# A two-layer diffusion trunk on one core: the large inputs re-laid by the host as the loads read them, and the tokens given transposed

## The chip, the cores and the metric

The kernel runs on one core of one Trainium2 chip. The metric is the device time of one execution in microseconds (us); the kernel before takes 2646.81 us, the median of 3 runs. The core has a matmul engine, TensorE (PE in the profile, with PEld for its weight loads), a vector engine (DVE), a scalar engine (ACT), GpSimd (POOL) and SyncE (SP), which here issues the DMAs. Each of them takes its own instructions in the order in which they were laid down when the program was built.

## The reference

Two layers over 512 latent tokens `x` and 256 context tokens `ctx`, each a vector of 2048. The first ("even") layer holds differential attention (8 heads) and windowed attention with a sink (8 heads), the second ("odd") one attention with normed queries and keys (8 heads) and latent attention (8 heads). Cut to what matters:

```python
silu_c = jax.nn.silu(c); silu_cc = jax.nn.silu(c_ctx)
for l in range(DEPTH):                                   # DEPTH = 2
    mod = silu_c @ w_mod[l] + b_mod[l]                   # 2048 -> 6144, one vector
    shift, scale, gate = jnp.split(mod[:, None, :], 3, axis=-1)
    cmod = silu_cc @ w_mod[l] + b_mod[l]                 # the same for the context
    cshift, cscale, cgate = jnp.split(cmod, 3)
    h = rmsnorm(x, norm_g[l]) * (1.0 + scale) + shift
    hc = rmsnorm(cx, norm_g[l]) * (1.0 + cscale) + cshift
    u, uc = h @ w_in, hc @ w_in                          # e_w_in or o_w_in
    ...                                                  # two groups of attention heads
    y = jnp.concatenate([y1, y2], axis=-1) * jax.nn.silu(ug)
    x = x + gate * (y @ w_o[l])                          # and cx likewise in the first layer
return rmsnorm(x, final_g)
```

## The kernel before

**Layout.** Activations are kept transposed: 2048 features are 16 chunks of 128 partitions, and a chunk is a tile of 128 x 768 whose first 512 columns are the latent tokens and whose last 256 are the context. Each float32 operand of a large product is split into two narrower parts (a cast on ACT, L273 for weights, and a subtraction on DVE, L231), and each row block of a projection is three matmuls (L292, L293, L295), each over 512 and 256 columns. A weight piece goes from DRAM through `wraw` (L278, the load at L282, three buffers of 128 x 1024) and `wsplit` (L265) to `proj` (L297). A load takes a block of 128 columns and up to 8 x 128 rows of a weight as it lies in DRAM, so each contiguous run is 128 floats, 512 bytes.

**Start.** The tokens come as rows of x and ctx: 24 loads of 128 x 512 (L321), 2 KB a row. ACT squares each and sums it along the row (L324). PE transposes the tiles, 96 blocks of 128 x 128 (L331), and DVE copies them out of PSUM into the 16 transposed tiles `xT` (L334, L336). Those are also written to the scratch tensors `x0d` in DRAM, two of them early (L339) and 14 at the end of the start (L429), since the residual of the first layer is read from there (`out_chunk`, L698). From the sums comes the reciprocal root (L342 to L344), which `spread` (L239) turns, by matmuls with the identity (L236), into a row `rs0` that all partitions hold.

**Modulation.** `mod_first(k)` (L131) makes scale and shift of chunk k of the first layer on PE: w_mod comes in pieces of 128 columns (L149, 512 bytes a row), 32 matmuls (L153) on four column groups of the array, a copy on ACT (L160), and two tiny matmuls (L163) that add up the groups; DVE adds the bias (L122, L126). It runs two chunks ahead of the loop at L415, which for each chunk makes the normed and modulated input (`make_h`, L383: the product with rs0 on POOL or DVE, h on ACT L390, an affine step on DVE L393, and the lower part l by L231) and does 24 matmuls of the first four projection blocks. Chunk 0's modulation waits for nothing but its loads. All other gates, scales and shifts come from `mod_later` (L168), in the background: 128 loads of 128 x (2 x 512) of w_mod (L175, 2 KB a row), multiplied and summed on DVE (L186), ACT (L181, L183) and POOL (L184), and folded by PE (L194) with narrow matmuls. `tick` (L223) lets a few of its 128 pieces go between the heads. Its raw tiles `mraw` have two buffers.

**Order.** The source gives the order of dependencies; when the program is built, a scheduler picks from what is ready and so sets each engine's order. All loads and stores go through SP's queue in the order of their issue; a DMA whose buffer is still being read holds those behind it.

**Later norms.** In `out_chunk` ACT squares the new tokens (L710), POOL adds them up (L715), and `rstd_cols` (L251) sums over the partitions by matmuls against a column pair of ones (L256), six for a 128 x 768 tile. The last part of the odd layer has `d_pe` (L868), with two loads of 64 columns, and the shared rotary key (L861), a projection of 64 columns that is written to both halves of the partitions.

Of the kernel before, what the change touches and what calls it, by code (L numbers as in the profile page):

```python
# [9 lines left out]
F32 = mybir.dt.float32  # L10
# [7 lines left out]
P = 128  # L18
# [14 lines left out]
O_G0 = 2368  # L33
# [8 lines left out]
def trunk_kernel(ctx: ExitStack, tc: tile.TileContext, T):  # L42
# [39 lines left out]
    x0d = [dr.tile([P, TOK], F32, name=f"x0d{j}") for j in range(NCH)]  # L82
# [36 lines left out]
    def mod_finish(l, k0, nk, src, nv=2):  # L119
        """adds the bias to chunks k0.. of the modulation; the scale becomes (1 + scale) * norm_g"""  # L120
# [10 lines left out]
    def mod_first(k):  # L131
        """scale and shift of one chunk of the first layer on the tensor engine"""
        acc = pst.tile([P, 512], F32, name="T")
        for sec in range(2):
            col = D_MODEL * (1 - sec) + 128 * k
            at = 0
            while at < NCH:
# [6 lines left out]
                else:  # L144
# [4 lines left out]
                last_raw[0] = nc.sync.dma_start(rv, T["w_mod"][0][128 * at:128 * (at + n), col:col + P]  # L149
                                                .rearrange("(k p) c -> p k c", p=P))  # L150
# [82 lines left out]
    def spread_to(dst, cols, ts):  # L233
        """per-token columns (every other one) to a row that every partition holds"""
# [16 lines left out]
    def rstd_cols(accs, ts, dim, name, bank=jbank):  # L251
        """1 / rms over the partitions, one column pair for each tile of tokens"""
# [12 lines left out]
    def wsplit(rv, nk, cols=P):  # L265
        """the rows of a loaded weight piece, each as an exact sum of two narrower parts"""
        res = []
        for k0 in range(0, nk, 4):
# [3 lines left out]
            for c in range(0, P, cols):  # L272
                nc.scalar.copy(wh[:, :n, c:c + cols], rv[:, k0:k0 + n, :])  # L273
                sub(wl[:, :n, c:c + cols], rv[:, k0:k0 + n, :], wh[:, :n, c:c + cols])
# [3 lines left out]
    def wraw(src, nk, cols=P, raw=None):  # L278
# [3 lines left out]
        nc.sync.dma_start(rv, src.rearrange("(k p) c -> p k c", p=P))  # L282
# [14 lines left out]
    def proj(w, col, xs=None, lat_only=False, cols=P, at=(0, 512)):  # L297
# [4 lines left out]
        for k0 in range(0, n, 8):  # L302
            nk = min(8, n - k0)
            ws = wsplit(wraw(w[128 * k0:128 * (k0 + nk), col:col + cols], nk, cols), nk, cols)
# [5 lines left out]
    def xrows(t, d0):  # L310
        if t < 4:
            return T["x"][0, 128 * t:128 * t + 128, d0:d0 + 512]
        return T["ctx"][0, 128 * (t - 4):128 * (t - 4) + 128, d0:d0 + 512]

    ssx = const.tile([P, 6, 4], F32, name="ssx")
    xT = []
    for dg in range(4):
        xt = []
        for t in range(6):
            a = hslot("xin", F32)[:, 0:512]  # L320
            nc.sync.dma_start(a, xrows(t, 512 * dg))  # L321
            xt.append(a)
            sq = sp["ep"].tile([P, 512], F32, tag="sqA", name="sqx", bufs=1)
            nc.scalar.activation(sq, a, AF.Square, accum_out=ssx[:, t, dg:dg + 1])  # L324
        for i in range(4):
            k = 4 * dg + i
            xk = hslot("xT", F32) if k == 0 else tmp("xT") if k == 1 else slot("xT") if k < 12 else (oslot if k < 14 else sgslot)("xT")
            for t0, t1 in ((0, 4), (4, 6)):
                tp = psj.tile([P, 512], F32, name="J")
                for t in range(t0, t1):  # L330
                    nc.tensor.transpose(out=tp[:, 128 * (t - t0):128 * (t - t0) + 128],  # L331
                                        in_=xt[t][:, 128 * i:128 * i + 128], identity=ident)
                if t0 == 0:
                    nc.vector.tensor_copy(xk[:, 0:512], tp)  # L334
# [6 lines left out]
    rsv = rsx.rearrange("p (a b) -> p a b", b=2)[:, :, 0]
    nc.vector.reduce_sum(rsv, ssx, axis=AX.X)  # L342
    nc.scalar.activation(rsv, rsv, AF.Sqrt, bias=epsc, scale=1.0 / D_MODEL)
    nc.vector.reciprocal(rsv, rsv)  # L344
# [3 lines left out]
    # constants of the even layer  # L348
# [34 lines left out]
    def make_h(l, k, xk, rs, xn, first):  # L383
        """normed and modulated input, split; first: which factor is there early, the norm's or the modulation's"""
# [688 lines left out]
```

## Time and profile before

| what | us |
|---|---|
| median of 3 runs | 2646.81 (2646.05 to 2647.2) |
| profiled execution, span | 2642.8 |
| outside the span (median less span) | 4.0 |
| PE busy | 2522.8 (95%) |
| DVE busy | 1653.1 (63%) |
| ACT busy | 1169.6 (44%) |
| POOL busy | 510.7 (19%) |
| first projection matmul | 45.71 |
| last matmul of the start's projections | 177.64 |

The DMA engines moved 303.39 MB at 115 GB/s over the whole span. The profile is a page on one execution, and a trace that can be asked by stretch, line or tile. Its rows give, in this order, the line of the kernel, the engine, the operation, what is written and from what, the count, and then busy us, the mean ns of one, and the idle time before it with what ended it. PEclk is the clock that TensorE was granted, 1.0 being full. A float32 matmul shows as two records in the timeline. A chain is followed back from the last instruction; here it goes back to about 1154 us and says nothing of the start, which is read from the stretches.

### The profile page before, as it was taken

The numbers are of one execution on the slowest core, as the hardware profiler recorded it, in microseconds if no ns is written. First come the engines' busy times: TensorE is split into PE (matmuls) and PEld (weight loads), VectorE is DVE, ScalarE is ACT, GpSimd is POOL, SyncE is SP. The second block draws the span as 40 slices with busy tenths as digits, with TensorE's granted clock in tenths as the row PEclk, the third lists the DMA queues.
The fourth block names the chain that finished last, engine by engine and source line by source line (L and its number), as shares of the span: only waits on it lengthen the run. The fifth ranks groups of instructions, "written<-read, shape, count | busy, mean of one in ns | idle before, by whom it ended". The sixth has DMA issues, their size and how long they took to land.

```text
span 2642.8 us, 38799 instructions
## 1 busy us (share of the span) xinstructions
PE 2522.8 (95%) x14830; PEld 2124.4 (80%) x14830; DVE 1653.1 (63%) x3199; ACT 1169.6 (44%) x2500; POOL 510.7 (19%) x340
## 2 busy tenths in 40 slices
PE   6989999999999989999998999899999999999998
PEld 4767887888788878888887888688888888777787
DVE  4458666556855688777756665767745336776634
ACT  4234544444544455544444333345434335554433
POOL 0114000001301164443402443310010010000010
PEclk9999999999999999999999999899999999999999
DMA  9993111111311244343443554635622232122334
GB/s 286 279 271 112 47 47 48 47 54 47 112 50 59 64 143 120 108 132 104 130 132 116 181 181 149 193 112 161 186 68 84 68 92 58 51 77 72 88 114 149
DMA packets 394553, 303.39 MB, mean 115 GB/s; under 512 B 18048, under 2 KB 334464, under 8 KB 394368
## 3 DMA queue, kind: packets, MB, share of 16 engines
q1 hardware_dynamic: 394368, 300.93, 38.2%
q8 instruction: 116, 1.90, 0.3%
q14 instruction: 69, 0.57, 0.1%
HBM read 268.64 MB, written 32.24 MB: 114 GB/s over the span
## 4 chain that ended last, share of the span: by engine, by line
PE 47%; DVE 5%; DMA 2%; ACT 1%; issue 1%; POOL 0%; ACTq 0%; SPq 0%; DVEq 0%; POOLq 0%
PE J L292 12%; PE J L295 12%; PE J L293 12%; PE O L579 3%; PE SL L512 3%; PE SC L507 2%; PE T L564 2%; DMA mraw<-in_w_mod_dram 1%; DVE macc L186 1%; DVE l L396 1%; DVE wl L231 1%; PE T L256 0%; PE J L194 0%; POOL macc L184 0%; DVE ptl L231 0%
## 5 line engine op out<-in xcount | busy, mean ns | idle before, releaser
L292 PE MATMUL J<-h,wh 128*128 128x512 f32 (+1 forms) x2224 | 788.3, 357 | 9.4 <-ACT h L390 5.0
L293 PE MATMUL J<-l,wh 128*128 128x512 f32 (+1 forms) x2224 | 769.3, 355 | 4.3 <-DVE l L396 3.4
L295 PE MATMUL J<-h,wl 128*128 128x512 f32 (+1 forms) x2224 | 710.9, 356 | 3.3 <-DVE wl L231 3.3
L231 DVE TENSOR_TENSOR wl<-wraw,wh 128x512 fp32r<-128x512 f32 (+1 forms) x504 | 394.1, 787 | 327.9 <-ACT wh L273 312.0
L273 ACT CAST wh<-wraw 128x512 fp32r<-128x512 f32 (+1 forms) x496 | 302.8, 615 | 536.9 <-PE J L293 471.4
L292 PEld LDWEIGHTS J<-h,wh 128*128 128x128 f32 x2224 | 423.9, 191 | 86.3 <-ACT h L390 6.7
L293 PEld LDWEIGHTS J<-l,wh 128*128 128x128 f32 x2224 | 425.3, 191 | 59.5 <-DVE l L396 4.6
L295 PEld LDWEIGHTS J<-h,wl 128*128 128x128 f32 x2224 | 391.3, 192 | 37.9 <-DVE wl L231 5.1
L184 POOL TENSOR_TENSOR macc<-macc,mraw 128x512 f32<-128x512 f32 x180 | 267.0, 1484 | 266.1 <-ACT mraw L183 233.7
L292 PE MATMUL J<-yh,wh 128*128 128x512 f32 (+1 forms) x800 | 275.1, 351 | 5.2 <-ACT yh L473 4.1
L293 PE MATMUL J<-yl,wh 128*128 128x512 f32 (+1 forms) x800 | 272.4, 351 | 0.2
L186 DVE SCALAR_TENSOR_TENSOR macc<-mraw,silc,macc 128x512 f32<-128x512 f32 x240 | 235.3, 980 | 50.9 <-DMA mraw<-in_w_mod_dram 46.9
L295 PE MATMUL J<-yh,wl 128*128 128x512 f32 (+1 forms) x800 | 252.9, 349 | 0.0
L183 ACT ACTIVATE mraw<-mraw,silc 128x512 f32<-128x512 f32 x180 | 129.8, 724 | 203.0 <-DVE macc L186 178.5
L568 ACT CAST pth<-T 128x256 fp32r<-128x256 f32 (+2 forms) x288 | 125.6, 450 | 149.8 <-PE T L564 146.4
L292 PEld LDWEIGHTS J<-yh,wh 128*128 128x128 f32 x800 | 150.3, 189 | 33.2 <-ACT yh L473 4.9
L231 DVE TENSOR_TENSOR ptl<-T,pth 128x256 fp32r<-128x256 f32 (+2 forms) x288 | 145.4, 516 | 42.9 <-ACT pth L568 40.5
L293 PEld LDWEIGHTS J<-yl,wh 128*128 128x128 f32 x800 | 150.9, 189 | 20.0 <-DVE yl L231 1.1
L523 DVE TENSOR_REDUCE mc<-SC 128x1 f32<-128x256 f32 x208 | 87.3, 420 | 118.4 <-PE SC L507 117.6
L440 POOL TENSOR_TENSOR r<-r,cos 128x512 f32<-128x512 f32 x31 | 40.7, 1313 | 581.9 <-DVE t L439 386.7
L295 PEld LDWEIGHTS J<-yh,wl 128*128 128x128 f32 x800 | 140.2, 190 | 12.4
L538 ACT ACTIVATE e<-SC,nb 128x256 f32<-128x256 f32 x144 | 68.2, 474 | 184.9 <-DVE nb L532 128.8
(297 smaller groups left out, 3789.2 us busy)
## 6 DMA issues: line engine op xcount, KB each, us to landing
mraw<-in_w_mod_dram SPq DMA_DIRECT2D x164, 512.0 KB, 4.1
wraw<-in_e_w_in_dram SPq DMA_DIRECT2D x96, 512.0 KB, 3.8
wraw<-in_w_o_dram SPq DMA_DIRECT2D x62, 512.0 KB, 4.1
wraw<-in_o_w_in_dram SPq DMA_DIRECT2D x62, 512.0 KB, 3.9
mraw<-in_w_mod_dram SPq DMA_DIRECT2D x28, 384.0 KB, 6.3
x0d<-xT SPq DMA_DIRECT2D x16, 384.0 KB, 6.4
res<-x0d SPq DMA_DIRECT2D x16, 384.0 KB, 4.7
xad<-nx SPq DMA_DIRECT2D x16, 384.0 KB, 2.4
```

Source lines behind the costliest of these rows:

```text
L183: nc.scalar.mul(rv[:, i, :], rv[:, i, :], sc)
L184: nc.gpsimd.tensor_tensor(macc[:, v, :], macc[:, v, :], rv[:, i, :], op=ALU.add)
L186: nc.vector.scalar_tensor_tensor(macc[:, v, :], rv[:, i, :], sc, macc[:, v, :], op0=ALU.mult, op1=ALU.add)
L231: nc.vector.tensor_tensor(o, a, h.bitcast(F32), op=ALU.subtract)
L273: nc.scalar.copy(wh[:, :n, c:c + cols], rv[:, k0:k0 + n, :])
L292: nc.tensor.matmul(o, lhsT=wh, rhs=xh[:, c0:c1], start=first and (opens or o is lat), stop=False)
L293: nc.tensor.matmul(o, lhsT=wh, rhs=xl[:, c0:c1], start=False, stop=False)
L295: nc.tensor.matmul(o, lhsT=wl, rhs=xh[:, c0:c1], start=False, stop=last and (closes or o is lat))
L512: nc.tensor.matmul(SL[:, c0:512], lhsT=q, rhs=k[:, 128 * lo:128 * hi], start=(i == 0), stop=(i == n - 1 and not masks))
L523: nc.vector.reduce_max(mc, SC[:, :256], axis=AX.X)
L568: nc.scalar.copy(ph, tv)
L579: nc.tensor.matmul(o, lhsT=v[:, cols[i]], rhs=pt[part][:, i, :], start=(n == 0), stop=(n == len(steps) - 1))
```

## The change

The host now lays the large inputs out as the loads read them, and the loads become plain rows.

- `xT` is the transposed x and ctx, 16 tiles of 128 x 768: 16 loads with rows of 3 KB take the place of 24, and transposes, PSUM copies, row sums and all of `x0d` (two early writes, 14 late ones) go. `out_chunk` reads its residual from `xT`.
- The sums of squares now come from the transposed tiles: ACT squares each (128 x 768) and PE sums it over the partitions with six matmuls against a column pair of ones, 96 in all. Root and reciprocal follow for 12 columns.
- `wm0` holds the modulation's first part by chunk and section, so a piece is a row of 2, 3 or 4 KB; `wm1` holds 128 x 1024 for one piece of `mod_later`, 4 KB a row.
- `_columns` lays `w_o`, `e_w_in`, `o_w_in` and `d_w_q_b` by blocks of 128 columns, so that a load of 8 row blocks has rows of 4 KB and one of 4 row blocks 2 KB; `dkv` has 4 KB.
- The 64 columns of the shared rotary key stand twice in `ow`, so that all pieces have 128 columns and `wsplit`, `wraw` and `proj` lose `cols`; the gates' first column moves from 2368 to 2432. `d_pe` makes one load instead of two.

```diff
-                last_raw[0] = nc.sync.dma_start(rv, T["w_mod"][0][128 * at:128 * (at + n), col:col + P]
-                                                .rearrange("(k p) c -> p k c", p=P))
+                last_raw[0] = nc.sync.dma_start(raw[:, :n * P], T["wm0"][k, sec][:, at * P:(at + n) * P])
...
-                nc.sync.dma_start(rv, T["w_mod"][l][256 * r:256 * r + 256, 512 * b:512 * b + 512]
-                                  .rearrange("(k p) c -> p k c", p=P))
+                nc.sync.dma_start(raw, T["wm1"][b + 4 if l else b - 8, r])
...
-        rv = raw[:, :nk * cols].rearrange("p (k c) -> p k c", k=nk)
-        nc.sync.dma_start(rv, src.rearrange("(k p) c -> p k c", p=P))
-        return rv
+        nc.sync.dma_start(raw[:, :nk * P], w[col // P][:, k0 * P:(k0 + nk) * P])
+        return raw[:, :nk * P].rearrange("p (k c) -> p k c", k=nk)
...
-    ssx = const.tile([P, 6, 4], F32, name="ssx")
-            a = hslot("xin", F32)[:, 0:512]
-            nc.sync.dma_start(a, xrows(t, 512 * dg))
-            nc.scalar.activation(sq, a, AF.Square, accum_out=ssx[:, t, dg:dg + 1])
-                    nc.tensor.transpose(out=tp[:, 128 * (t - t0):128 * (t - t0) + 128],
-                                        in_=xt[t][:, 128 * i:128 * i + 128], identity=ident)
-                    nc.vector.tensor_copy(xk[:, 0:512], tp)
-                    nc.vector.tensor_copy(xk[:, 512:768], tp[:, :256])
-                nc.sync.dma_start(x0d[k], xk)
+    mp = jbank()
+    for k in range(NCH):
...
+        nc.sync.dma_start(xk, T["xT"][k])
+        xT.append(xk)
+        sq = sp["ep"].tile([P, TOK], F32, name="e")
+        nc.scalar.square(sq, xk)
         for t in range(6):
+            nc.tensor.matmul(mp[:, 2 * t:2 * t + 2], lhsT=sq[:, P * t:P * t + P], rhs=ones[:, 0:2],
+                             start=(k == 0 and t == 0), stop=(k == NCH - 1 and t == 5))
...
         load_cs(64)
-        for k in range(2, NCH):
-            nc.sync.dma_start(x0d[k], xT[k])
...
-        nc.sync.dma_start(res, x0d[j])
+        nc.sync.dma_start(res, T["xT"][j])
...
-    kr = roped(*proj(w, D_KPE0, cols=64), 64)
+    kr = roped(*proj(w, D_KPE0), 64)
...
+def _columns(w):
+    r, c = w.shape
+    return np.ascontiguousarray(w.reshape(r // P, P, c // P, P).transpose(2, 1, 0, 3)).reshape(c // P, P, r)
```

How the change stands in the instruction order is seen at three places. First PE at the very start. `cid` holds the identity, `xin` the token rows, `e` (in the third row of after) the squares, `mraw` pieces of w_mod, and `rsx` the reciprocal roots. Before:

```order
L98 MATMUL T<-cid,e 128x89
L101 MATMUL T<-cid,e 128x96
L331 MATMUL J<-cid,xin 128x128 x94
L153 MATMUL T<-mraw_529,sil 32x128 x6
L331 MATMUL J<-cid,xin 128x128 x2
L236 MATMUL J<-cid,rsx 128x128 x4
L153 MATMUL T<-mraw_537,sil 32x128 x6
L236 MATMUL J<-cid,rsx 128x128 x2
```

And after:

```order
L97 MATMUL T<-cid,e 128x89
L100 MATMUL T<-cid,e 128x96
L314 MATMUL J<-ones,e 128x2 x96
L150 MATMUL T<-mraw_398,sil 32x128 x6
L150 MATMUL T<-mraw_406,sil 32x128 x6
L150 MATMUL T<-mraw_414,sil 32x128 x4
L150 MATMUL T<-mraw_420,sil 32x128 x3
L232 MATMUL J<-cid,rsx 128x128 x6
```

The 96 matmuls of the sums stand where the transposes stood, all in one row, and chunk 0's modulation behind them.

Second, DVE at the last chunk of the start: `l0_14` and `l0_15` are the lower parts of chunks 14 and 15, `modc0` the scales and shifts, `macc` the sum of the background modulation. Before:

```order
L231 TENSOR_TENSOR l0_14_1885<-xn_1882,h0_14_1884 128x768
L122 TENSOR_TENSOR modc0_205<-T_1810,bmod_186 128x2 x2
L126 SCALAR_TENSOR_TENSOR modc0_205<-modc0_205,vcol_185 128x2
L393 TENSOR_SCALAR xn_1915<-xn_1915,modc0_205 128x512
L393 TENSOR_SCALAR xn_1915<-xn_1915,modc0_205 128x256
L231 TENSOR_TENSOR l0_15_1918<-xn_1915,h0_15_1917 128x768
```

And after:

```order
L227 TENSOR_TENSOR l0_14_1754<-xn_1751,h0_14_1753 128x768
L182 SCALAR_TENSOR_TENSOR macc_2659<-mraw_2660,silc_177,macc_2659 128x512
L121 TENSOR_TENSOR modc0_189<-T_1679,bmod_170 128x2 x2
L125 SCALAR_TENSOR_TENSOR modc0_189<-modc0_189,vcol_169 128x2
L182 SCALAR_TENSOR_TENSOR macc_2659<-mraw_3303,silc_177,macc_2659 128x512 x2
L367 TENSOR_SCALAR xn_1784<-xn_1784,modc0_189 128x512
L367 TENSOR_SCALAR xn_1784<-xn_1784,modc0_189 128x256
L227 TENSOR_TENSOR l0_15_1787<-xn_1784,h0_15_1786 128x768
```

Three multiply-adds of the background modulation now stand ahead of l0_15.

Third, SP's queue at the end of the start, from the last loads of the first modulation on. Before:

```order
L149 DMA mraw_1859<-in_w_mod_dram 128x8x128
L371 DMA cos64_1948<-in_cos64_dram 128x512
L371 DMA sin64_1950<-in_sin64_dram 128x512
L429 DMA x0d2_95<-xT_256 128x768
L429 DMA x0d3_96<-xT_267 128x768
L429 DMA x0d4_97<-xT_302 128x768
```

And after:

```order
L147 DMA mraw_1728<-in_wm0_dram 128x1024
L345 DMA cos64_1817<-in_cos64_dram 128x512
L345 DMA sin64_1819<-in_sin64_dram 128x512
L172 DMA mraw_2660<-in_wm1_dram 128x1024
L172 DMA mraw_3303<-in_wm1_dram 128x1024
L172 DMA mraw_4078<-in_wm1_dram 128x1024
```

Before, 14 writes of x0d stand between the last of these and the first load of the background modulation; after, its loads follow at once.

More of the change, by code (lines that the diff above doesn't have):

```diff
@@ L32 @@
 D_CQ0, D_CKV0, D_KPE0 = 1536, 2048, 2304
-O_G0 = 2368
+O_G0 = 2432
 LAM_INIT = 0.2
@@ L80, in hslot @@
         return hp.tile([P, TOK], dt, tag="hT", name=name)
-    x0d = [dr.tile([P, TOK], F32, name=f"x0d{j}") for j in range(NCH)]
     x1d = [dr.tile([P, SEQ], F32, name=f"x1d{j}") for j in range(NCH)]
@@ L262, in rstd_cols, with wsplit @@
         return rs
[L265 removed]
+    def wsplit(rv, nk):
         res = []
@@ L271, in wsplit, with wraw @@
             wl = wp.tile([P, 4, P], F32R, name="wl", bufs=4)
-            for c in range(0, P, cols):
-                nc.scalar.copy(wh[:, :n, c:c + cols], rv[:, k0:k0 + n, :])
-                sub(wl[:, :n, c:c + cols], rv[:, k0:k0 + n, :], wh[:, :n, c:c + cols])
+            nc.scalar.copy(wh[:, :n, :], rv[:, k0:k0 + n, :])
+            sub(wl[:, :n, :], rv[:, k0:k0 + n, :], wh[:, :n, :])
             res += [(wh[:, i, :], wl[:, i, :]) for i in range(n)]
         return res
-    def wraw(src, nk, cols=P, raw=None):
+    def wraw(w, col, k0, nk, raw=None):
         if raw is None:
             raw = wp.tile([P, 1024], F32, name="wraw", bufs=3)
-        rv = raw[:, :nk * cols].rearrange("p (k c) -> p k c", k=nk)
-        nc.sync.dma_start(rv, src.rearrange("(k p) c -> p k c", p=P))
-        return rv
+        nc.sync.dma_start(raw[:, :nk * P], w[col // P][:, k0 * P:(k0 + nk) * P])
+        return raw[:, :nk * P].rearrange("p (k c) -> p k c", k=nk)
     def mm_step(lat, cx, wk, xk, first, last, opens=True, closes=True, at=(0, 512)):
@@ L303, in proj @@
             nk = min(8, n - k0)
-            ws = wsplit(wraw(w[128 * k0:128 * (k0 + nk), col:col + cols], nk, cols), nk, cols)
+            ws = wsplit(wraw(w, col, k0, nk), nk)
             for i in range(nk):
@@ L340, in trunk_kernel @@
     rsx = sm.tile([P, 12], F32, name="rsx", bufs=2)
[L341 to L344, printed above, removed]
+    nc.scalar.activation(rsx, mp[:, :12], AF.Sqrt, bias=epsc, scale=1.0 / D_MODEL)
+    nc.vector.reciprocal(rsx, rsx)
     rs0 = sp["ep"].tile([P, TOK], F32, name="e")
@@ L400, in make_h @@
         return h, lo
-    w = T["e_w_in"][0]
+    w = T["ew"]
     s_start = (sbank("SC"), sbank("SL"))
@@ L420, in trunk_kernel @@
                 raw = sm.tile([P, 2, 512], F32, name="macc", bufs=1).rearrange("p a b -> p (a b)") if i == 3 else None
-                ws4[i] = wsplit(wraw(w[128 * k:128 * k + 512, start_cols[i]:start_cols[i] + P], 4, raw=raw), 4)
+                ws4[i] = wsplit(wraw(w, start_cols[i], k, 4, raw), 4)
             next(nxt, None)
@@ L728, in trunk_kernel @@
             if k % 8 == 0:
-                ws4[j] = wsplit(wraw(wo[128 * k:128 * k + 1024, 128 * j:128 * j + P], 8), 8)
+                ws4[j] = wsplit(wraw(wo, 128 * j, k, 8), 8)
             mm_step(two[j], two[2][:, 256 * j:256 * j + 256], ws4[j][k % 8], ys[k], k == 0, k == NCH - 1,
@@ L736, in trunk_kernel @@
     tick(96 - due[1])
-    w = T["o_w_in"][0]
+    w = T["ow"]
     rs1 = etile("rs1")
@@ L751, in trunk_kernel @@
             if k % 4 == 0:
-                ws4[i] = wsplit(wraw(w[128 * k:128 * k + 512, odd_cols[i]:odd_cols[i] + P], 4), 4)
+                ws4[i] = wsplit(wraw(w, odd_cols[i], k, 4), 4)
             mm_step(lat, cx, ws4[i][k % 4], hT[k], k == 0, k == NCH - 1, opens=(i % 2 == 0), closes=(i % 2 == 1))
@@ L863, in trunk_kernel @@
     cqn = [split(t, 512, hslot, "cq") for t in cq]
-    wq = T["d_w_q_b"][0]
-    wkv = T["d_w_kv_b"][0]
+    wq = T["dq"]
+    wkv = T["dkv"]
     def d_pe(p2):
-        raw = wp.tile([P, 1024], F32, name="wraw", bufs=3)
-        rv = raw[:, :512].rearrange("p (k c) -> p k c", k=4)
-        for u in range(2):
-            c0 = 192 * (2 * p2 + u) + 128
-            nc.sync.dma_start(rv[:, :, 64 * u:64 * u + 64], wq[:, c0:c0 + 64].rearrange("(k p) c -> p k c", p=P))
-        ws = wsplit(rv, 4)
+        ws = wsplit(wraw(wq, 128 * (8 + p2), 0, 4), 4)
         ps = psj.tile([P, 512], F32, name="J")
@@ L963, in trunk_kernel @@
             if k % 4 == 0:
-                ws4[j] = wsplit(wraw(wo[128 * k:128 * k + 512, 128 * j:128 * j + P], 4), 4)
+                ws4[j] = wsplit(wraw(wo, 128 * j, k, 4), 4)
             mm_step(three[j], None, ws4[j][k % 4], ys[k], k == 0, k == NCH - 1)
@@ L1021, with _packed @@
 _VECS = ["c", "c_ctx", "norm_g", "a_sub_g", "c_q_g", "c_k_g", "d_q_a_g", "d_kv_a_g", "final_g"]
-_INS = ["x", "ctx", "w_mod", "w_o", "e_w_in", "a_lam_q1", "a_lam_k1", "a_lam_q2", "a_lam_k2", "b_sink", "o_w_in",
-        "d_w_q_b", "d_w_kv_b"]
+_INS = ["a_lam_q1", "a_lam_k1", "a_lam_q2", "a_lam_k2", "b_sink"]
+def _columns(w):
+    r, c = w.shape
+    return np.ascontiguousarray(w.reshape(r // P, P, c // P, P).transpose(2, 1, 0, 3)).reshape(c // P, P, r)
+def _packed(inputs):
+    g = {n: np.asarray(inputs[n]) for n in ("x", "ctx", "w_mod", "w_o", "e_w_in", "o_w_in", "d_w_q_b", "d_w_kv_b")}
+    res = {"xT": np.concatenate([g["x"][0].T, g["ctx"][0].T], axis=1).reshape(NCH, P, TOK)}
+    wm = g["w_mod"].reshape(2, NCH, P, 3, NCH, P)
+    res["wm0"] = wm[0][:, :, 1::-1].transpose(3, 2, 1, 0, 4).reshape(NCH, 2, P, D_MODEL)
+    wm = g["w_mod"].reshape(2, 8, 2, P, 12, 512).transpose(0, 4, 1, 3, 2, 5).reshape(2, 12, 8, P, 1024)
+    res["wm1"] = np.concatenate([wm[0, 8:], wm[1]])
+    res["wo"] = np.stack([_columns(w) for w in g["w_o"]])
+    res["ew"] = _columns(g["e_w_in"][0])
+    w = g["o_w_in"][0]
+    kpe = w[:, D_KPE0:D_KPE0 + 64]
+    res["ow"] = _columns(np.concatenate([w[:, :D_KPE0], kpe, kpe, w[:, D_KPE0 + 64:]], axis=1))
+    w = g["d_w_q_b"][0].reshape(512, 8, 192)
+    res["dq"] = _columns(np.concatenate([w[:, :, :P].reshape(512, -1), w[:, :, P:].reshape(512, -1)], axis=1))
+    res["dkv"] = g["d_w_kv_b"][0].reshape(2, P, 4, 512).transpose(2, 1, 0, 3).reshape(4, P, 1024)
+    return {n: np.ascontiguousarray(a) for n, a in res.items()}
 def _angles(dim):
```

32 lines of the change are left out of this document (7 added, 25 removed).

## The prediction

> **What bounds the kernel now.** The page of the profile comes first, for the span, the engines, the clock granted to TensorE and the DMA share by slices, and the chain that ended last.
>
> ```profile
> span 2642.8 us, 38799 instructions
> ...
> PE   6989999999999989999998999899999999999998
> ...
> PEclk9999999999999999999999999899999999999999
> DMA  9993111111311244343443554635622232122334
> ...
> PE 47%; DVE 5%; DMA 2%; ACT 1%; issue 1%; POOL 0%; ACTq 0%; SPq 0%; DVEq 0%; POOLq 0%
> PE J L292 12%; PE J L295 12%; PE J L293 12%; PE O L579 3%; PE SL L512 3%; PE SC L507 2%; PE T L564 2%; DMA mraw<-in_w_mod_dram 1%; DVE macc L186 1%; DVE l L396 1%; DVE wl L231 1%; PE T L256 0%; PE J L194 0%; POOL macc L184 0%; DVE ptl L231 0%
> ```
>
> TensorE holds nearly every slice at 9, and a slice is 66 us. The change takes few matmuls away, so it can gain only where PE waits. The first slice shows PE at 6, the next ones DMA at 9: there the start runs, about 180 us. The rest of the chain is matmuls, with 1 part in 50 on DMA.
>
> Next I cut the time into stretches and asked for the busy time of each engine (us, then PE, PEld, DVE, ACT and POOL busy, PEclk, DMA share, GB/s).
>
> ```profile
> 45.70:178.00 132.30, 117.69 (x1340) 93.25 (x1340) 54.59 (x116) 36.85 (x68) 14.95 (x8) 0.97 1.09 294
> 180.00:240.00 60.00, 52.77 (x268) 43.32 (x267) 57.48 (x73) 29.83 (x55) 35.10 (x23) 0.93 0.46 140
> 925.00:1320.00 395.00, 364.89 (x2207) 324.39 (x2206) 304.95 (x504) 200.17 (x477) 187.02 (x125) 0.96 0.40 122
> ```
>
> From 45.7 to 178 the first projection blocks run in step with the modulation. The DMA share is 1.09: the queues are full throughout, at 294 GB/s, and PE idles 132.3 − 117.7 = 14.6 us. After that the DMA engines are half free. The DMA view for 40 to 160 us says how the bytes come, the one for 160 to 182 what happens when the rows get longer (the writes of x0d have rows of 3 KB, the loads of w_mod rows of 512 bytes). The waits of PE up to 260 us, of SP's queue up to 200, and of DVE after 178 say who suffers.
>
> ```profile
> DMA packets 67092, 33.85 MB, mean 282 GB/s; under 512 B 1347, under 2 KB 67079, under 8 KB 67079
> ```
> ```profile
> GB/s 321 337 322 295 287 293 289 291 290 291 293 318 358 383 406 421 417 391 397 408 413 425 397 413 425 417 408 408 419 413 413 419 413 413 413 419 413 393 257 331
> ...
> x0d<-xT SPq DMA_DIRECT2D x14, 384.0 KB, 6.4
> ```
> ```profile
> PE T L153 <- DMA mraw<-in_w_mod_dram: 14.9, 19, 2.8
> ```
> ```profile
> SPq L149 <- PE T L153: 18.8, 12, 3.7
> SPq L282 <- DVE wl L231: 13.5, 8, 6.8
> ```
> ```profile
> DVE macc L186 <- DMA mraw<-in_w_mod_dram: 46.9, 38, 3.7
> ```
>
> So short rows move at 282 GB/s, long ones at 413, and PE waits 14.9 us for w_mod. The Trainium skill ("DMA: Bandwidth & Descriptors", Specifications) says that a transfer of 512 bytes or more already reaches line rate, by which longer rows would bring nothing; this trace does not agree, with 282 against 413 GB/s.
>
> **The start, before the first projection.** Before, x comes as rows, PE transposes it, and the first projection matmul is at 45.71 us. The timeline of ACT and PE gives the first arrival and the end of the head; the last row is chunk 0's modulation.
>
> ```profile
> 5.61 0.63 ACT L324 ACTIVATE sqx<-xin 128x512 f32<-128x512 f32 x1 [1.35 <-DMA xin<-in_x_dram]
> ```
> ```profile
> 42.54 0.61 PE L163 MATMUL T<-cid,e 128*128 128x2 f32 x4
> 43.08 1.06 PE L153 MATMUL T<-mraw,sil 128*32 128x128 f32 x20
> 45.71 0.50 PE L292 MATMUL J<-h,wh 128*128 128x512 f32 x1 [1.56 <-ACT h L390]
> ```
> ```profile
> L331 PE MATMUL J<-cid,xin 128*128 128x128 f32 x96 | 19.9, 347 | 9.8 <-DMA xin<-in_x_dram 7.1 <-DMA xin<-in_ctx_dram 1.7 <-DVE xT L334 0.5
> ```
>
> The change removes those 96 transposes (19.9 us of PE) with the PSUM copies and the reduction, and puts 96 f32 matmuls of 128x2 in their place (sum of squares over partitions), one for each of 6 token blocks of 16 tiles, all ahead of the modulation on PE. What such a matmul costs shows at 1656 us, where the second layer's norm does the same thing twelve records (six matmuls) at a time, and where a spread follows:
>
> ```profile
> 1656.04 1.39 PE L256 MATMUL J<-ones,acc 128*128 128x2 f32 x12
> 1658.53 2.72 PE L256 MATMUL J<-ones,sq 128*128 128x2 f32 x12 [1.10 <-ACT sq L710]
> 1661.88 2.93 PE L236 MATMUL J<-cid,rsx 128*128 128x128 f32 x12 [0.62 <-DVE rsx L261]
> ```
> ```profile
> L710 ACT ACTIVATE sq<-nx x15: 842/846/848, 1417.0 to 1657.6; 128x768 f32<-128x768 f32 x15
> ```
> ```profile
> 952.10:955.50 3.40, 3.40 (x17) 3.40 (x18) 2.89 (x6) 0.66 (x2) 0.49 (x1) 0.50 0.58 172
> 1658.50:1661.80 3.30, 2.72 (x12) 2.63 (x12) 0.56 (x3) 0.27 (x1) 0.00 (x0) 0.50 1.02 325
> 16.84:20.25 3.41, 2.61 (x8) 1.47 (x9) 0.69 (x1) 3.28 (x9) 0.00 (x0) 0.50 1.03 395
> 23.70:27.00 3.30, 2.15 (x17) 1.45 (x14) 2.46 (x5) 2.81 (x9) 0.00 (x0) 1.00 1.03 342
> ```
>
> So six cost 1.39 us at the full clock and 2.72 at half. Which one here? At 16.84 the clock is at half, and PE, with nothing but 128x128 transposes, has it back at 23.70. At 1658.5 and at 952.1 narrow matmuls filled 82 and 100% of a stretch as long as the clock's own steps (3.4 us), and the clock stood at 0.50 through it; the spread with 128 columns came after. I take half: the narrow matmuls do not bring the clock back. Then the sixteen tiles cost 16 × 2.72 = 43.5 us. A tile of 384 KB at 413 GB/s comes every 0.95 us and its square takes 0.85, so PE sets the pace. The first square begins at 5.9 (5.61, and 0.3 for 384 KB instead of 256) and ends at 6.8; 6.8 + 43.5 = 50.3. Then chunk 0's modulation, 64 records, cold, from these rows:
>
> ```profile
> 64.18 3.26 PE L153 MATMUL T<-mraw,sil 128*32 128x128 f32 x52 [0.33 <-DMA mraw<-in_w_mod_dram]
> ```
> ```profile
> 109.71 2.32 PE L153 MATMUL T<-mraw,sil 128*32 128x128 f32 x64
> ```
>
> 3.26 / 52 × 64 = 4.0, the spread 2.9, 44 records of chunk 1 that stand before the tiny matmuls (2.32 / 64 × 44 = 1.6), and 3.2 from there to the first projection (42.54 to 45.71), of which 1.06 are matmuls that I have counted: 50.3 + 4.0 + 2.9 + 1.6 + 2.1 = 61 us. That is 15 later than before; the weights' loads, which before came last, have long landed.
>
> **The start, projections.** One chunk's 24 matmuls and the end of the last chunk:
>
> ```profile
> 52.71 0.86 PE L292 MATMUL J<-h,wh 128*128 128x512 f32 x3
> ...
> 56.77 0.28 PE L295 MATMUL SL<-h,wl 128*128 128x256 f32 x1
> ```
> ```profile
> 177.64 0.28 PE L295 MATMUL SL<-h,wl 128*128 128x256 f32 x1
> ```
> ```profile
> L163 PE MATMUL T<-cid,e 128*128 128x2 f32 x64 | 8.8, 241 | 0.0
> ```
>
> Without a wait a chunk costs 57.0 − 52.7 = 4.3 us of projection, 2.3 of modulation and 0.5 of the tiny pair: 16 × 4.3 + 14 × 2.8 = 108. The 117.7 busy of before is 9.7 more, from windows at half clock and matmuls that start up after a wait; with fewer waits I keep half, 5. Of the idle 14.6 the DMA wait goes almost wholly: a chunk brings 2.36 MB (33.85 MB are 14.3 chunks), 8.4 us at 282 GB/s but 5.7 at 413, against 7.2 to 7.9 of PE. I keep 3.5 for it and 2 for waits on ACT and DVE. New is that three multiply-adds of the background modulation (980 ns class, L182 after) stand on DVE ahead of the last chunk's l0_15, two of them on a load issued after the last modulation load; about 1.7. 108 + 5 + 3.5 + 2 + 1.7 = 120, so this stage ends at 61 + 120 = 181 instead of 177.9: +3. It gives back nearly all that it loses.
>
> **After the start.** From 180 to 240 DVE is busy 57.5 of 60 and PE idles 7.2. The multiply-adds that moved forward and the 14 writes of x0d that no longer precede the first background load take some of it: −2. Further on DVE waits 46.9 us for mraw in 38 waits. How their transfers stand from 925 to 1320:
>
> ```profile
> mraw<-in_w_mod_dram SPq DMA_DIRECT2D x53, 512.0 KB, 3.7
> wraw<-in_e_w_in_dram SPq DMA_DIRECT2D x30, 512.0 KB, 4.0
> ```
>
> A weight piece ahead of one in the queues now takes 512 KB / 413 = 1.3 us instead of 1.9, so such a wait gets 0.2 to 0.5 shorter; the chain holds 1% of them, and off the chain they are free. −3, with ends at 0 (all covered by PE's own work) and −12. The weight loads (wraw) are hardly ever waited for, so their longer rows earn nothing directly. The 64-column pieces that become 128 columns cost PE nothing, since a matmul's time goes with its moving columns, and save a few casts: 0, between −1 and +1. Residuals read from the input instead of x0d: 0, the load is as long.
>
> The sum against the profiled execution: 2642.8 + 3 − 2 − 3 = 2641; the time outside the span (2646.8 − 2642.8 = 4.0) is added as before, so 2645. I put it at 2644, since the start's waits could all go. Its own range is 2634 to 2654: −5 if the clock is still full for the first tiles, +5 if the start keeps its 9.7, −9 to +3 for the middle.
>
> **Rivals.** First, the clock comes back after one full window even with narrow matmuls. Then a tile costs 1.39: 6.8 + 22.2 = 29 instead of 50.3, modulation and spread some 3 less, but 2 given back to transfers that have less time to run ahead: −22, 2622 us. For it: 1656.04 shows 1.39 right behind wide matmuls; against it, 952.1 and 1658.5. The Trainium skill ("TensorE: Matmul & The Clock Gate", Part 1) says that one busy window of about 3.4 us brings the full clock, which would be this rival; at 952.1 the trace does not agree, with PE 100% busy at 0.50.
>
> Second, the one that ends on the other side: the start waits for buffers, not for bytes. SP's queue stands 18.8 us on L153 (a buffer still read) and 13.5 on L231, and in-order issue holds the loads behind. If chunks keep the pace of before, the head's +15 stays: 2644 + 12 = 2656, or 2658 with a little more. It decides from about 0.7 us of wait left per chunk, where 1.06 (14.9 / 14) was. Against it: the DMA share of 1.09 without a gap.
>
> Third, the middle gains more: 0.7 us on most of the 38 waits, and the chain holds half of them: −13, 2631.
>
> That the rows stay slow (the change doing nothing for the rate) is the second again, with the same price.
>
> **Numbers.** 0.64 for the forecast, 0.12 for each of the three. 0.2% is 5.3 us, about what a measurement can tell here; the bounds are 2641.5 and 2652.1. Faster: 0.12 + 0.12 + 0.21 of the forecast's own range; slower: 0.12 + 0.07; within: 0.36. The range leaves out part of each end: 2619 to 2657, which is wide because of the clock.
>
> **What would show it.** After: L314 at 2.7 us a tile and PEclk 0.5 until about 50 us (1.3 and full: first rival); first projection near 61; PE's waits for mraw in the start under 4 us and a DMA share below 1 (second rival if over 10 and the queue never idle); the start over at about 181; waits of the background multiply-adds for mraw near 38 us instead of 46.9. I am wrong if the start ends below 165 or above 188, or the middle moves by more than 10.

## The result, and the profile after

The changed kernel takes 2655.9 us (median of 5 runs, 2653.27 to 2656.78) against 2646.05 of the kernel before (5 runs, 2642.07 to 2647.2): 1.0033 times as long, with a 95% interval of 1.002 to 1.0045. It is slower by about 10 us. Two later measurements, each beside the kernel before on the same chip, gave 1.0049 (1.0033 to 1.0065) and 1.0032 (1.002 to 1.0045).

The page of the changed kernel, the same parts as before:

```profile
span 2651.8 us, 38870 instructions
...
PE   8988999999999998989998999899999999999998
...
PEclk9999999999999999999999999899999999999999
DMA  7862111111311143343343554534522221122234
```

The first slice shows PE at 8 where it was 6, and the first three have DMA at 7, 8 and 6 where they had 9: the queues are less full, as the long rows should make them, PE is busier, and the span is 9.0 us longer. Where it got longer is found by laying the same instruction of both timelines side by side: one matmul of the attention early in the program and one late. First before, then after:

```profile
353.68 0.28 PE L579 MATMUL O<-pth,vh 128*128 128x256 f32 x1
...
2303.14 0.49 PE L579 MATMUL O<-ptl,vh 128*128 128x256 f32 x2
```

```profile
362.74 0.28 PE L551 MATMUL O<-pth,vh 128*128 128x256 f32 x1
...
2311.68 0.48 PE L551 MATMUL O<-ptl,vh 128*128 128x256 f32 x2
```

At 354 us the changed kernel is 9.1 us behind, at 2303 us 8.5, at the end 9.0. Between these two executions all of the loss arises in the start; the time behind it gives back nothing and loses nothing. The start itself, in PE's timeline after:

```profile
6.26 41.12 PE L314 MATMUL J<-ones,e 128*128 128x2 f32 x192 [2.31 <-ACT e L312]
47.30 2.35 PE L150 MATMUL T<-mraw,sil 128*32 128x128 f32 x38
49.59 2.93 PE L232 MATMUL J<-cid,rsx 128*128 128x128 f32 x12
...
56.78 0.96 PE L287 MATMUL J<-h,wh 128*128 128x512 f32 x3 [0.58 <-ACT h L364]
...
180.92 0.79 PE L288 MATMUL J<-l,wh 128*128 128x512 f32 x1 [4.31 <-DVE l L227]
...
186.31 0.27 PE L290 MATMUL SL<-h,wl 128*128 128x256 f32 x1
```

And the stretch of the first projections (us, then PE, PEld, DVE, ACT and POOL busy, PEclk, DMA share, GB/s), PE's waits for the modulation's loads up to 260 us (all of them in this stretch), the same for the stretch of the kernel before (45.7 to 178 us), and SP's longest wait after:

```profile
56.80:186.60 129.80, 118.34 (x1340) 93.22 (x1340) 61.87 (x120) 39.57 (x73) 20.89 (x13) 0.96 0.80 271
```
```profile
PE T L150 <- DMA mraw<-in_wm_dram: 5.1, 6, 2.6
```
```profile
PE T L153 <- DMA mraw<-in_w_mod_dram: 11.9, 16, 2.8
```
```profile
SPq L147 <- PE T L150: 60.6, 17, 11.8
```

The sums of squares hold PE from 6.3 to 47.4 us without a gap. The first projection comes at 56.8 instead of 45.7: 11.1 us later. The stretch from there to the end of the stage takes 129.8 instead of 132.3, so only about 2.4 come back. In two more profiles of the changed kernel it takes 133.8 and 131.5, so what comes back lies between nothing and 2.4. PE's waits for loads in the stretch fell from 11.9 to 5.1 us, and SP now stands 60.6 us, where it stood 18.8, on buffers that PE still reads: its loads have become early. But PE's busy time, 118.3, is not below the 117.7 of before, and a wait of 4.3 us for the last chunk's lower part is new.

The end of the stage in DVE's timeline, after:

```profile
174.77 2.36 DVE L182 SCALAR_TENSOR_TENSOR macc<-mraw,silc,macc 128x512 f32<-128x512 f32 x2 [0.83 <-DMA mraw<-in_wm_dram]
177.05 1.81 DVE L367 TENSOR_SCALAR xn<-xn,modc 128x512 f32<-128x512 f32 x2
178.89 1.97 DVE L227 TENSOR_TENSOR l<-xn,h 128x768 fp32r<-128x768 f32 x1
```

Two of the multiply-adds of the background modulation stand right ahead of the last chunk's steps, as the order showed. And these steps take twice what they take for chunk 14 in the same timeline (0.90 us at 169.32 for the two of L367 and 0.96 at 170.26 for the subtraction). Two additions of the background run on POOL beside them (2.82 us from 177.23 on).

### The profile page after: what moved, and what is told of

The parts are those of the page before. It is cut to its first block, busy times and chain, and to the rows that moved or that the text cites. A ratio compares the mean times of both kernels' runs of the same rounds, so it can differ in the third digit from the quotient of the medians.

```text
span 2651.8 us, 38870 instructions
## 1 busy us (share of the span) xinstructions
PE 2543.4 (96%) x14926; PEld 2150.6 (81%) x14926; DVE 1639.7 (62%) x3162; ACT 1166.3 (44%) x2464; POOL 513.5 (19%) x340
## 5 line engine op out<-in xcount | busy, mean ns | idle before, releaser
L227 DVE TENSOR_TENSOR wl<-wraw,wh 128x512 fp32r<-128x512 f32 x500 | 396.4, 797 | 322.8 <-ACT wh L268 313.4
L268 ACT CAST wh<-wraw 128x512 fp32r<-128x512 f32 x492 | 302.5, 618 | 541.7 <-PE J L288 487.1
L182 DVE SCALAR_TENSOR_TENSOR macc<-mraw,silc,macc 128x512 f32<-128x512 f32 x240 | 234.5, 977 | 51.0 <-DMA mraw<-in_wm_dram 45.3
```

Of the source, the lines that this page charges most:

```text
L182: nc.vector.scalar_tensor_tensor(macc[:, v, :], rv[:, i, :], sc, macc[:, v, :], op0=ALU.mult, op1=ALU.add)
L227: nc.vector.tensor_tensor(o, a, h.bitcast(F32), op=ALU.subtract)
L268: nc.scalar.copy(wh[:, :n, :], rv[:, k0:k0 + n, :])
```

## The experiments

The theory after the result: the loss is the head's, where 96 narrow matmuls run at a half clock and one after another; what the head loses is passed on, since the stage behind is PE's own work. Rivals: the stage behind takes back any shorter head (loads, buffers); the loss is the wait at the stage's end; the long rows themselves earn nothing or cost.

**Wider products.** 80 columns of ones instead of 2.

```diff
-            nc.tensor.matmul(mp[:, 2 * t:2 * t + 2], lhsT=sq[:, P * t:P * t + P], rhs=ones[:, 0:2],
+            nc.tensor.matmul(mp[:, 80 * t:80 * t + 80], lhsT=sq[:, P * t:P * t + P], rhs=ones[:, 0:80],
```

> The changed kernel, with 80 columns of ones in place of 2 in the 96 matmuls of the sums (the root reads the first two of each 80). Theory (the head decides: narrow matmuls leave the clock at half, and what the head loses is passed on to the end one for one): a tile's six matmuls fall from 2.57 us to about 1.45 after a first cold window, the sums end at about 31 instead of 47, the first projection matmul comes at about 40 instead of 56.8, and the time falls by about 16 to 2640. First rival (the stage behind is bound by its loads and buffers and takes a shorter head back in waits): the first projection comes at 40 too, but the stage still ends near 186 and the time stays at 2655. Second rival (such matmuls are slow for another reason than the clock, as their weight loads): a tile stays at 2.6 us or gets longer, and the time stays at 2655 or rises.

Measured: 1.0035 of before (1.002 to 1.0049), no gain. The kernel was run once more for its timeline.

> The kernel with 80 columns of ones once more, for a profile, since the first one fell in a disturbed execution. Its time (1.0035 of before, no better than the changed kernel) says that the theory failed or that the gain was taken back. If wide matmuls do bring the full clock, a tile takes about 1.45 us, the first projection is at about 40 and the loss lies in the stage behind; if the clock stays at half or the wider matmuls cost as much as the clock wins, a tile stays at 2.5 us or more and the first projection near 57.

The timeline of PE, and the loads and products of the line:

```profile
6.08 41.25 PE L314 MATMUL J<-ones,e 128*128 128x80 f32 x192 [2.08 <-ACT e L312]
47.26 2.00 PE L150 MATMUL T<-mraw,sil 128*32 128x128 f32 x38
49.19 1.60 PE L232 MATMUL J<-cid,rsx 128*128 128x128 f32 x12
```
```profile
L314 PEld LDWEIGHTS J<-ones,e x192: 288/333/338, 6.1 to 46.8; 128*128 128x128 f32 x192
```

In the changed kernel the same line reads:

```profile
L314 PEld LDWEIGHTS J<-ones,e x192: 285/333/333, 6.3 to 47.0; 128*128 128x128 f32 x192
```

Wider products up to 80 columns earn nothing. Forty times as many columns take 41.25 us instead of 41.12: 215 ns and 214 ns a record. The pace goes with the weight load, whose stationary operand is the tile of squares; the runs don't separate the load from a fixed cost of each product. And it is the half clock's: in the kernel before, such a load takes 333 ns at 1658.5 us, where PEclk is 0.50, and 192 ns at 1656, where it is 1.00. So 80 columns don't bring the full clock either. (PEclk gives 1.00 for this stretch of the changed kernel, but the trace's first clock record comes at 53 us; the pace tells the clock here, the column doesn't.) That no width would bring it is not shown. In the kernel before, the spread at 1661.88 has 128 columns behind each of 12 such loads of 333 ns, and the clock came back behind it:

```profile
1661.90:1665.30 3.40, 2.90 (x12) 2.61 (x12) 1.37 (x3) 0.00 (x0) 0.00 (x0) 0.50 0.96 322
1665.30:1668.70 3.40, 1.18 (x5) 0.78 (x5) 2.56 (x3) 1.79 (x4) 3.21 (x2) 1.00 1.03 369
```

**The squares added on DVE.** PE then has six matmuls instead of 96.

```diff
-        for t in range(6):
-            nc.tensor.matmul(mp[:, 2 * t:2 * t + 2], lhsT=sq[:, P * t:P * t + P], rhs=ones[:, 0:2], ...)
+        if k > 1:
+            nc.vector.tensor_tensor(ssq, ssq, sq, op=ALU.add)
```

> The changed kernel, with the 16 squared tiles added up on DVE (128x768 each) and only six narrow matmuls at the end. Theory (the head decides): the squares follow the transfers (about 1 us a tile), the sums are there at about 28 instead of 47, the first projection comes at about 37, and the time falls by about 19 to 2637. First rival (loads and buffers behind): the first projection at about 37, the stage still ends near 186, time 2655.

Measured: 0.9987 of before (0.9971 to 1.0002). PE's timeline, its waits, and the stage of the projections:

```profile
25.93 2.72 PE L320 MATMUL J<-ones,ssq 128*128 128x2 f32 x12 [22.11 <-DVE ssq L317]
...
41.99 1.65 PE L287 MATMUL J<-h,wh 128*128 128x512 f32 x3 [1.72 <-ACT h L369]
```
```profile
PE T L150 <- DMA mraw<-in_wm_dram: 11.6, 11, 3.4
PE SC L484 <- DVE qa L227: 3.1, 1, 3.1
PE J L288 <- DVE l L227: 2.9, 1, 2.9
```
```profile
41.99:179.63 137.64, 122.19 (x1337) 96.39 (x1338) 59.58 (x120) 40.11 (x72) 20.50 (x12) 0.93 0.76 259
```

The sums are there at 28.6 and the first projection comes at 42.0, 14.8 us earlier. It doesn't come at 37: on ACT three casts of weights stand ahead of the first h and wait 4.4 us for their loads (1.54, 1.66 and 1.20). The time falls by 0.45 to 0.6% against the changed kernel's three measurements, 12 to 16 us where 19 were forecast (10.0 by the profiled spans). So the head's loss is real, and most of it is passed on; whether one for one, these numbers don't settle. The stage takes 137.6 us instead of 129.8: with 15 us less to run ahead, the loads are waited for again, 11.6 us, and the clock is lower (PEclk 0.93 instead of 0.96), with PE 122.2 us busy instead of 118.3. The rival holds for that part.

**The operands exchanged.** Ones are the weights, squares move.

```diff
+        for mp, c0, c1 in zip(mps, (0, 512), (512, 768)):
+            nc.tensor.matmul(mp[:, :c1 - c0], lhsT=ones, rhs=sq[:, c0:c1], start=(k == 0), stop=(k == NCH - 1))
```

> The changed kernel with the operands of the sums exchanged: the 128 x 128 ones are the weights, the squares move through (512 and 256 columns), so every partition gets every token's sum and the spread by matmuls goes; root and reciprocal then run over 768 columns. Theory (the 2.57 us of a tile are six weight loads of squares at half clock, which moving 2 or 80 columns does not change, and only moving columns bring the clock back): after two windows at half clock a tile takes about 1.5 us, the sums are there at about 34 instead of 47, the first projection at about 42, and the time falls to about 0.999 of before (some 10 below the changed kernel). Rival (the clock stays at half at the start whatever PE does, or the products themselves are as slow): a tile takes 2.6 us or more, the sums end at 47 or later, and the time stays at 1.004.

Measured: 0.9988 (0.9977 to 1.0). PE's timeline, the loads, and what follows the sums on DVE and POOL:

```profile
6.49 19.20 PE L314 MATMUL J<-e,ones 128*128 128x512 f32 x52 [2.16 <-ACT e L312]
...
26.91 1.56 PE L314 MATMUL J<-e,ones 128*128 128x512 f32 x4
...
44.26 1.65 PE L287 MATMUL J<-h,wh 128*128 128x512 f32 x3 [5.06 <-ACT h L361]
```
```profile
L314 PEld LDWEIGHTS J<-e,ones x64: 186/190/337, 6.5 to 31.8; 128*128 128x128 f32 x64
```
```profile
32.68 4.96 DVE L318 RECIPROCAL e<-e 128x512 f32<-128x512 f32 x2 [7.09 <-ACT e L317]
...
37.90 4.39 DVE L227 TENSOR_TENSOR wl<-wraw,wh 128x512 fp32r<-128x512 f32 x2 [0.17 <-ACT wh L268]
```
```profile
37.73 4.01 POOL L356 TENSOR_TENSOR xn<-xT,e 128x768 f32<-128x768 f32 x2 [37.28 <-DVE modc L121]
```

As the theory had it: 1.5 us a tile, and a weight load of the same shape takes 190 ns instead of 333. The sums are there at 32.4 instead of 47.4. From there to the first projection it takes 11.9 us (9.4 in the changed kernel), so that comes at 44.3, not 42: the reciprocal over 768 columns takes 5 us, and then two subtractions for the weights take 4.4 us on DVE, 0.68 each at 43.29 and 43.89, while POOL works on its products. The time is 12 to 16 us below the changed kernel's, a little more than forecast. How long PE is busy does not decide the clock alone: the Trainium skill ("TensorE: Matmul & The Clock Gate", Part 1) counts one busy window of about 3.4 us, and here 41 us of nothing but weight loads with 2 or 80 columns behind each did not do it, while 512 and 256 columns did (the first clock record of this trace, at 10.9 us, is full). That moving columns are what counts fits all of these rows; whether it is their number or their share of the time, no run separates.

**The background's multiply-adds behind the last chunk.**

```diff
+                        with tc.issue_after(last_lo[0].ins) if (l, b) == (0, 8) else nullcontext():
                             nc.vector.scalar_tensor_tensor(macc[:, v, :], rv[:, i, :], sc, macc[:, v, :],
```

> The changed kernel, with the first multiply-adds of the background modulation queued on DVE behind the last chunk's lower part instead of ahead of it. If the 4.3 us wait for it and the half clock that follows (some 2 us) are a loss of their own, the time falls by about 6 to 2650 and the stage ends at about 180 instead of 186.6. If DVE only does the same work later, where PE waits for it then, the wait goes and the time stays within 2 of 2655.

Measured: 1.0049 (1.0033 to 1.0064), no gain; and as the chips differ, once more beside the changed kernel:

> The changed kernel with the first multiply-adds behind the last chunk's lower part, beside the changed kernel on the same chip. If the wait of 4.3 us and the half clock behind it cost time, it is 4 to 6 us faster than the changed kernel (0.15 to 0.25%). If the stage's gain is lost again behind, the two are within 0.1%.

> The changed kernel, as the measure for the one with the multiply-adds moved: 1.0033 to 1.0049 of before.

> The changed kernel once more, on the chip of the others of this call, as their measure: 1.0033 times the kernel before (its first measurement), 10 us by the span.

Measured: 1.0035 (1.0023 to 1.0047) with the edit and 1.0032 (1.002 to 1.0045) without, side by side; 1.0049 (1.0033 to 1.0065) without at another time. PE's timeline with the edit, the end of the stage and one attention matmul early and one later; then the same without; then the stage of the projections with and without:

```profile
181.45 0.28 PE L292 MATMUL SL<-h,wl 128*128 128x256 f32 x1
184.61 1.54 PE L459 MATMUL J<-cid,ev 128*128 128x128 f32 x6 [2.88 <-ACT ev L453]
...
359.32 0.28 PE L553 MATMUL O<-pth,vh 128*128 128x256 f32 x1
...
1821.26 0.28 PE L553 MATMUL O<-pth,vh 128*128 128x256 f32 x1
```
```profile
181.66 0.79 PE L288 MATMUL J<-l,wh 128*128 128x512 f32 x1 [4.00 <-DVE l L227]
...
187.10 0.28 PE L290 MATMUL SL<-h,wl 128*128 128x256 f32 x1
...
362.06 0.28 PE L551 MATMUL O<-pth,vh 128*128 128x256 f32 x1
...
1820.85 0.28 PE L551 MATMUL O<-pth,vh 128*128 128x256 f32 x1
```
```profile
55.90:181.73 125.83, 115.49 (x1340) 91.21 (x1340) 55.95 (x114) 35.80 (x65) 17.78 (x11) 0.99 0.80 271
```
```profile
55.85:187.38 131.53, 117.95 (x1340) 93.28 (x1340) 61.46 (x120) 39.62 (x73) 21.13 (x13) 0.96 0.79 267
```

The wait is gone and the stage is 5.7 us shorter. But PE then waits 2.9 us for a copy on ACT (0.7 without the edit); at 360 us 2.7 are left of the gain, at 1821 none (0.4 behind). So the wait at the end of the stage doesn't cost all that its row says: about half of the gain is lost again at once. Which wait takes the last 3 us the traces don't settle; and with intervals of some 3 us to each side, the times would not show a gain of 2.7.

**The rows alone.** The first modulation's loads with short rows in the changed kernel; then the kernel before with long rows everywhere and its own token path; then the kernel before with long rows for the first modulation and nothing else.

```diff
-                last_raw[0] = nc.sync.dma_start(raw[:, :n * P], T["wm0"][k, sec][:, at * P:(at + n) * P])
+                last_raw[0] = nc.sync.dma_start(rv, T["w_mod"][0][128 * at:128 * (at + n), col:col + P]
+                                                .rearrange("(k p) c -> p k c", p=P))
```

> The changed kernel, with the first modulation's loads from w_mod as it lies (512 bytes a row) and everything else as changed. If the longer rows earned what the waits show (11.9 us of PE's waits for these loads in the stage before, 5.1 after), the stage gets about 6 us longer and the time rises to about 2661. If PE's own work bounds the stage and the rows earned nothing, it stays at 2655; if they cost something it falls.

Measured: 1.0089 (1.0065 to 1.0113), slower by 0.4 to 0.6% than the changed kernel: 10 to 15 us where 6 were expected. The stage takes 142.0 us, PE waits 12.6 in it for these loads, and as with the summed squares the clock is lower too (PEclk 0.93).

> The kernel before, with the weights laid out by the host as in the changed one, but the tokens read as rows, transposed and staged as before: the long rows alone. If the first stage is bound by the rate of its loads, PE's waits for the modulation's loads fall from 11.9 us to about 5 and the time falls by 6 to 9 (0.997 of before). If it is bound by when buffers come free, the waits stay at 10 to 12, as they did with the short head of the summed squares (11.6), and the time stays within 3 of before.

Measured: 0.9954 (0.994 to 0.9969), the fastest of all. Its stage, and its waits up to 260 us:

```profile
43.70:167.10 123.40, 114.36 (x1340) 93.40 (x1340) 56.10 (x116) 36.60 (x68) 15.02 (x8) 0.97 0.89 311
```
```profile
PE T L151 <- DMA mraw<-in_wm_dram: 8.4, 8, 2.2
```

The stage takes 123.4 us instead of 132.3, and the first projection comes 2 us earlier. The waits fell a little less than expected (6.6 us of the 8.4 lie in the stage, 11.9 before, 5 expected), the time more: 12 us by this measurement, 10 by the one below.

> The kernel before with one edit: the first modulation's loads read long rows; all other weights and the tokens as before. If the long rows earn only where PE waits for them, in the first stage, this has all the gain of the long rows everywhere: 0.995 of before, within 0.15% of that kernel, which is timed beside it. If the rest of the kernel earns something from its long rows, it stays behind that kernel by 0.1% or more (3 us were forecast for the middle).

> The kernel before with long rows for all weights, once more as the measure for the run with one edit: 0.9954 of before.

Measured: 0.9962 (0.9949 to 0.9975) with the one edit and 0.9961 (0.9949 to 0.9972) with all rows long. The two are the same within some 3 us: the rows of all other weights earn nothing that shows. So the change holds a gain of about 0.4% (the first modulation's rows) and a loss of about 0.7% (the token path with all that hangs on it, 1.0032 less 0.9961). The head is not all of that loss: with the squares summed on DVE the first projection comes as early as here (42.0 us against 43.7 and 42.1 in the two profiles with all rows long), and that kernel is still 0.26 to 0.33% slower, its stage 137.6 us against 123.4 and 125.2.

**More buffers.** Pieces of the modulation in free activation slots, first with the squares on DVE, then in the kernel with long rows, then with the multiply-adds moved as well.

```diff
-                if sec == 0 and k < 14:
+                if (sec == 0 and k < 14) or (k % 2 == 0 and k < 10):
```

> The kernel with the squares summed on DVE, where every other early chunk of the modulation gets its second section in three pieces in free activation slots instead of the two buffers and the spare tile. If the stage waits for buffers, PE's waits for these loads fall from 11.6 us to under 5, and the time falls by 6 to 8 below that kernel's (to about 0.996 of before). If it waits for the rate, or if PE only gets busier by the same amount, the time stays at that kernel's 0.9987 of before.

Measured: 0.9969 (0.9956 to 0.9982), with 7.6 us of waits instead of 11.6. That points to buffers as a part of it, though the waits are not down to 5 and the intervals of the two kernels overlap.

> The kernel before with the weights' long rows (0.9954 of before) and, besides, the second section of chunks 2, 4, 6 and 8 of the first modulation in free activation slots. If what is left of PE's waits for these loads (8.4 us) is a matter of buffers, they fall by half and the time by about 3 to 0.994; if of the order or the rate of the transfers, it stays at 0.9954.

Measured: 0.9979 (0.9969 to 0.999), no gain and rather worse than 0.9954 and 0.9961, although the waits fell from 8.4 to 5.4. The expectation failed. The stage took 128.5 us instead of 123.4, since PE was busy 120.4 us in it instead of 114.4, with the clock nearly the same (PEclk 0.96 and 0.97); why is open.

> The kernel with the squares summed on DVE and the deeper buffers (0.9969 of before), with the first multiply-adds of the background modulation behind the last chunk's lower part. If the wait of 3.5 us for it and the half clock behind it are a loss of their own, the time falls by 4 to 6 to about 0.995. If what is gained there is lost again behind, as in the changed kernel with the same edit, it stays at 0.997.

Measured: 0.9971 (0.9961 to 0.9982), the same as without the moved multiply-adds. Here too that edit earns nothing that shows.

## Why the prediction was wrong

I forecast 2644, a little faster, and gave 0.19 to slower by over 0.2%; it is 10 us slower. By the profiled executions the forecast span was 2641 and the measured one 2651.8, 10.8 us more. The step that failed is the repayment: the stage of the projections was to give back 12 of the 15 us that the head loses, and the time behind it 5 more. The stage gave back about 2 and the time behind it nothing. Step by step:

- The head, "61 us". Measured 56.8, 4.2 less. The half clock was right and the price nearly (2.57 us a tile, not 2.72). The reason, that narrow products don't bring the clock back, holds for 2 and for 80 columns. What it missed is that the pace goes with the squares as weights: with the operands exchanged the price is 1.5 us.
- "Of the idle 14.6 the DMA wait goes almost wholly ... I keep 3.5 for it". Mis-sized: 5.1, 7.3 and 8.3 us in three profiles. The 14.9 us behind it were a misreading too: 3.0 of them lie ahead of the first projection, so the stage had 11.9 to lose, 0.85 a chunk instead of 1.06.
- "With fewer waits I keep half, 5" of PE's 9.7 us above the bare sum. This step failed. PE's busy time in the stage stayed at 118.3, 10.3 above the bare 108, and with the long rows alone it is still 114.4. A part is the clock. In these two stretches of the stage the granted clock was half, and PE was busy 8.7 us in them (6.7 in two such stretches before):

```profile
152.04:155.45 3.41, 3.41 (x44) 2.39 (x46) 0.65 (x2) 0.00 (x0) 0.00 (x0) 0.50 0.80 221
179.34:186.17 6.83, 5.25 (x17) 4.58 (x18) 5.63 (x8) 3.82 (x9) 1.02 (x2) 0.50 0.24 78
```

By an estimate, that all work takes twice as long at half clock, it costs 4.3 us of the 10.3 (3.4 of the 9.7 before). The rest is some 6 us in both kernels; what it is, no run shows.
- The end of the stage, "about 1.7". Mis-sized: 4.3 us of wait, and some 2.4 more since the last 18 products then ran at half clock (5.7 us from 180.92 on, against 3.3 for the same 18 of the chunk before; the 2.4 are in the busy time above). With the multiply-adds moved the stage is 5.7 us shorter. Left out of the sum were the multiply-adds' partners on POOL, beside which DVE's steps took 1.81 and 1.97 us. The Trainium skill ("SBUF — State Buffer", Terms, the shared port pair) has DVE and GpSimd exclude each other there for a whole instruction; the rows agree with it, no run here took POOL's additions away. That this wait costs the time is not shown: taking it away changed 1.0032 into 1.0035.
- The stage: "so this stage ends at 181". It ended at 186.6: 9.8 more in the stage (5.3 of PE's busy time, 118.3 for 113, and the rest idle time, 11.5 for 7.2), less 4.2 from the head.
- "After the start", −2 and −3. Neither came: the distance between the kernels is 8.7 us at the end of the stage, 9.1 at 354 and 9.0 at the end. The loads suggest why the middle earned nothing, from 925 to 1320 us after:

```profile
mraw<-in_wm_dram SPq DMA_DIRECT2D x55, 512.0 KB, 3.8
wraw<-in_ew_dram SPq DMA_DIRECT2D x31, 512.0 KB, 4.1
```

A piece lands after 3.8 and 4.1 us with rows of 4 KB, after 3.7 and 4.0 with rows of 2 KB and 512 bytes. So in this stretch, whose DMA share is 0.40, a transfer did not get shorter with its rows; I had worked with the rate of full queues (282 and 413 GB/s). Over the whole run DVE's waits for these loads went from 46.9 to 45.3 us, not to 38, by the group of its multiply-adds:

```profile
L182 DVE SCALAR_TENSOR_TENSOR macc<-mraw,silc,macc 128x512 f32<-128x512 f32 x240 | 234.5, 977 | 51.0 <-DMA mraw<-in_wm_dram 45.3 <-ACT macc L177 3.4
```

Of the rivals, the first (the clock comes back) is refuted by the 41 us. The second, slower because of buffers, had the time nearly exactly (2656) and its condition, that the chunks keep the pace of before, nearly too; but its reason is not borne out, so the number is luck as far as the runs show. Its mark was a wait of over 10 us for loads; the waits were 5.1 to 8.3, and the rest of the lost time lies in the end of the stage and in PE's busy time. Waits of over 10 came with a short head (11.6 with the squares on DVE) and with short rows (12.6).

Put together: 4.2 less in the head, 9.8 more in the stage and 5.3 more behind it make 10.9 of the 10.8. This is an account of two traces, and the stage alone differs by 4 us between profiles of the changed kernel; the end of the stage belongs to it, though a kernel without that wait was no faster by its time.

## What to carry to other kernels

Here a gain in bandwidth was worth something only where PE waits for loads in full queues: one of the seven re-laid weight tensors had all of the gain that shows. Removing staged transposes is no gain by itself; price what takes their place at the clock it will find, and ask of a reduction by matmul which operand is the weight: here the sums ended 15 us sooner with the large one on the moving side. A wait that goes is not yet time that is won: two edits (the moved multiply-adds, and the deeper buffers beside long rows) took waits away and the time stayed. A change of two parts with opposite signs is best timed in its parts: the rows alone made the kernel 0.4% faster, the whole change 0.3% slower.

## What the runs showed of the hardware

- A float32 weight load of 128 x 128 took 333 ns by its row at half clock and 190 at the full one. Matmuls with 2 or 80 moving columns behind such loads ran at 214 and 215 ns a record for 41 us, at half clock throughout. Twelve records with 128 columns behind such loads (2.9 us) brought the full clock back, and so did 512 and 256 columns, 4.4 us after the first of them.
- A reciprocal on DVE cost 5.0 us for 128 x 768 in two pieces, where the 12 columns of the changed kernel's root and reciprocal and the spread took 5.2 us together (47.3 to 52.5 in PE's timeline, with 2.3 of modulation in it).
- Two DVE subtractions of 128 x 512 took 4.4 us beside two POOL products of 128 x 768 (4.0 us), and 0.68 each right after.
- A 512 KB load landed in 3.7 to 4.1 us with rows of 512 bytes, 2 KB or 4 KB, where the DMA engines were 40% busy.
- The column PEclk shows 1.00 where no clock record lies, as in the first 50 us of the changed kernel.
